# Regrouping small matmuls in a two-layer attention trunk on one core: compression in one group, compressed scores by pairs of heads, narrow value products, a split output projection

## The chip, the core and the metric

The kernel runs on one core of a Trainium2 chip. TensorE (PE) multiplies matrices; VectorE (DVE), ScalarE (ACT) and GpSimd (POOL) do the element-wise work; SyncE (SP) issues most of the DMA transfers from queues that keep their order. The metric is the device time of one execution in microseconds (us), as the median of several runs.

## What is computed

The reference is a two-layer decoder trunk in float32 for 512 tokens of width 1024. Each layer projects its normalised input once and runs two attention mixers side by side, forgetting attention (FoX, 8 heads) and native sparse attention (NSA, 8 query heads over 2 kv heads), mixes them with per-channel gates, and ends in a squared-ReLU MLP. Cut to what the change touches:

```python
def compress_blocks(t, pos_emb, w1, b1, w2, b2):        # NSA: one key (value) per block of 32 tokens, step 16
    blocks = t[:, :, idx, :] + pos_emb
    flat = blocks.reshape(B, G, nc, CMP_BLOCK * dh)      # 2048 long; w1 is 2048 x 256
    return jax.nn.gelu(flat @ w1 + b1) @ w2 + b2

def fox_attention(q, k, v, log_f):                       # per head: causal, with a forget bias
    s = einsum(q, k) * scale + ci[..., :, None] - c[..., None, :]
    s = jnp.where(kpos[None, :] <= qpos[:, None], s, -jnp.inf)
    return softmax(s) @ v

# NSA, per query head: probabilities over the compressed blocks, over selected blocks, over a window
p_c = softmax(where(cmp_end <= qpos, einsum(q, kc) * scale, NEG_BIG)) * valid_c
...
y_a = from_heads(o_a) @ w_o_fox
y_b = from_heads(g0 * o_c + g1 * o_s + g2 * o_w) @ w_o_nsa
x = x + (sigmoid(gate_a) * y_a + sigmoid(gate_b) * y_b) @ w_out
```

## The kernel before

All activations are kept transposed: features on the 128 partitions, the 512 tokens along the free axis. A float32 product is made of three TensorE products of a type called fp32r, in `gemm` (lines 243 to 245): both operands are split into a high part (rounded by ACT) and a low part (the rest, by DVE), and high x high, high x low and low x high are summed in one bank of PSUM. Weights come as 512 KB transfers (`fetch`, L201) and are split by `convert` (L217 on ACT, L218 on DVE). The inputs `uh`, `ul` come from `make_u` (L265 on ACT, L266 on DVE); the sums of squares for the norm are made by `sumsq` (squares on ACT at L274, sums on POOL at L284) and finished in `rstd` (L298, L315), with plain float32 products.

A layer has stages: token projections (values and gates, L357 to L359), FoX attention, NSA attention, output projection, mix, MLP. In an attention stage `attend` walks through units, one for each head (FoX) or for each head and branch (NSA). A unit has the steps scores, transposes and values, and between steps the next products of a filler generator are issued, so that TensorE has projections to do while ACT and DVE make the softmax. The filler of FoX (`fill1`) holds the FoX projections of later pairs of heads, the projections of `kc` and `vc`, then `compress` alternating step by step with the remaining projections. The filler of NSA (`fill2`) holds gated output projections, `cmp_gen` (the compressed scores and probabilities) and the last query projections. In which order the instructions of each engine then stand is decided by a scheduler from the recorded program; each engine and each queue works through its order strictly.

- `compress`: the windows of `kc` and `vc` are copied into tiles `ca`, 16 row groups each; w1 of each is loaded by 8 transfers of 256 KB (L651, on SP's queue) into tiles of the tags `oh` and `ol`. Key and value products run in the two column halves of the array, so the tile of a product is 128 x 64 with 256 columns (L665); they are plain float32 and take two instructions each. The 32 products of a layer are made in chunks of 4 steps `jj` (8 products), with other work of the filler between chunks. The result goes through gelu and w2, and ends in the key block `kcz` (L712, L713) and the value block `vz`.
- `q_pair` and `k_pair`: `hilo` splits the scaled queries or keys of two heads into `hla` (high and low); transfers on SP (L397, L401, L410, L419) put them into `kda`, `q2a` and `qx` so that one product of 128 rows holds the high part of a head against high and low. POOL clears parts of `qx` (L417, L418).
- `cmp_probs` (L732): the compressed scores of the four heads of a kv head go to four groups of 32 rows in one PSUM bank. `kcz` holds the 32 block keys with zeros around; a shifted view places them in the rows of head r. Each head takes two products of 512 columns: 8 for a kv head.
- `values` of FoX (L490): the probabilities, transposed into blocks of 128 x 128, high part (`pth`) and low part (`ptl`), times the values `vf`. Of the four key blocks b, block 0 meets 512 query columns, block 1 384, block 2 256, and block 3 only the last 128; the tile of the third group holds 128 zero columns in front of block 3 (cleared by DVE at L471, L472), so that its product has 256 columns:

```python
todo = [(0, 0, 0, 512), (1, 1, 0, 384), (2, 2, 256, 256), (3, 2, 0, 256)]
```

- `out_half` and `out_pair` (L508, L509) gather the outputs of a pair of heads and split them into `oh`, `ol`; for NSA these are the inputs `yb[p]` of the output projection, `half(1, m, w)` for m = 0 to 7, four pairs of heads p each.

Of the kernel before, what the change touches and what calls it, by code (L numbers as in the profile page):

```python
# [11 lines left out]
F32 = mybir.dt.float32  # L12
# [7 lines left out]
T = 512  # L20
# [123 lines left out]
class Body:  # L144
# [259 lines left out]
    def q_pair(self, x, fox=False):  # L404

        hl = self.hilo(x, 0.125)
        q2 = self.t("q2", [128, 2, T], F32R)
        for e in range(2):
            for f in range(2):
                self.nc.sync.dma_start(q2[f * 64:(f + 1) * 64, e].bitcast(F32),  # L410
                                         hl[e * 64:(e + 1) * 64, f].bitcast(F32))
        if not fox:
            return q2
        qx = []
        for e in range(2):
            t = self.t(("oh", "ol")[e], [128, T], F32R, name="qx")
            self.nc.gpsimd.memset(t[64:128].bitcast(F32), 0.0)  # L417
            self.nc.gpsimd.memset(t[64:66].bitcast(F32), 1.0)  # L418
            self.nc.sync.dma_start(t[:64].bitcast(F32), hl[e * 64:(e + 1) * 64, 0].bitcast(F32))  # L419
            qx.append(t)  # L420
        return q2, qx
# [32 lines left out]
    def transposes(self, u):  # L454
# [3 lines left out]
        for g in range(3):  # L458
            ps = self.p("PT")
            if g < 2:  # L460
                todo = [(i, g) for i in range(g, NB)]
            else:
                todo = [(3, 3), (2, 2), (3, 2)]
# [4 lines left out]
            o = 0  # L468
            if g == 2:
                o = 128  # L470
                nc.vector.memset(h[:, :128].bitcast(F32), 0.0)  # L471
                nc.vector.memset(lo[:, :128].bitcast(F32), 0.0)  # L472
            nc.scalar.copy(h[:, o:o + n], ps[:, :n])
            nc.vector.tensor_sub(lo[:, o:o + n], ps[:, :n], h[:, o:o + n].bitcast(F32))
# [3 lines left out]
    def values(self, u):  # L478
        nc = self.nc
        if u.get("first", True):  # L480
            u["O"][0] = self.p("O")
        O = u["O"][0]
        first = u.get("first", True)
        pt = u["pt"]
        last = u.get("last", True)
        todo = [(0, 0, 0, 512), (1, 1, 0, 384), (2, 2, 256, 256), (3, 2, 0, 256)]
        for b, g, o, n in todo:
            v = u["v"](b)
            for f in range(2):
                nc.tensor.matmul(O[:, T - n:], v, pt[g][f][:, o:o + n],  # L490
                                 start=first and b == 0 and f == 0, stop=last and b == 3 and f == 1)
            yield
        if "after" in u:
            u["after"]()
# [132 lines left out]
    def compress(self, kc, vc, small, l):  # L627
# [3 lines left out]
        for x, pos in ((kc, "pos_k"), (vc, "pos_v")):  # L631
# [11 lines left out]
            yield  # L643
        hp = self.p("O")
        self.held = self.bank_o
        loaded = deque()

        def load(c):
            for i in range(2 if c < 8 else 0):
                raw = self.t(("oh", "ol")[i], [128, T], name="w1")  # L650
                nc.sync.dma_start(raw, a["w1"][l, i, c].rearrange("p j m -> p (j m)"))  # L651
                loaded.append(raw)

        load(0)
        load(1)
        for c in range(0, 8, 2):
            load(c + 2)
            yield
            load(c + 3)
            yield  # L660
            w = [loaded.popleft() for _ in range(4)]
            for j in range(4):
                jj = 2 * c + j
                for i in range(2):
                    nc.tensor.matmul(hp[64 * i:64 * i + 64, :256], A[i][jj // 8][:, jj % 8],  # L665
                                     w[j // 2 * 2 + i][:, j % 2 * 256:(j % 2 + 1) * 256],
                                     start=jj == 0, stop=jj == 15)
            yield
            yield
# [42 lines left out]
        nc.scalar.copy(self.kcz[:, :, 0, 96:128], k2)  # L712
        nc.vector.tensor_sub(self.kcz[:, :, 1, 96:128], k2, self.kcz[:, :, 0, 96:128].bitcast(F32))  # L713
# [10 lines left out]
    def cmp_probs(self, hk, q2):  # L724
# [4 lines left out]
        for r in range(4):  # L729
            q = q2[2 * hk + r // 2][:, r % 2]  # L730
            for f in range(2):
                nc.tensor.matmul(sc, self.kcz[:, hk, f, 96 - 32 * r:224 - 32 * r], q,  # L732
                                 start=r == 0 and f == 0, stop=r == 3 and f == 1)
# [41 lines left out]
    def setup(self, first):  # L775
# [13 lines left out]
        self.kcz = t[:, 512:1408].rearrange("p (h f n) -> p h f n", h=2, f=2)  # L789
# [71 lines left out]
    def layer(self, l, u):  # L861
# [49 lines left out]
        st = {}  # L911
# [7 lines left out]
        def fox_unit(h):  # L919
            p, e = divmod(h, 2)  # L920
            un = dict(q=lambda: st["qa", p][0][:, e], qx=lambda: st["qa", p][1][e], k=lambda: st["ka", p][e], O=[None],
# [3 lines left out]
            def after():  # L925
                if e == 0:
                    st["oa", p] = self.t("zz", [128, T], name="o")
                self.out_half(un["O"][0], st["oa", p], e)
                if e == 1:
                    st["oa", p] = self.out_pair(st["oa", p])  # L930
# [8 lines left out]
        def qproj(p):  # L939
            return proj(12 + p, ("qb", p), lambda ps: self.q_pair(self.roped(ps)))  # L940

        def cmp_gen(hk):
            yield from self.cmp_probs(hk, [st.get(("qb", p)) for p in range(4)])
# [101 lines left out]
        for m in range(8):  # L1045
            if m % 2 == 0:
                w = self.weights(a["wo"][l, 1, m // 2].rearrange("p i c -> p (i c)"))
            run(half(1, m, w))
# [456 lines left out]
```

## Time and profile before

| | us |
|---|---|
| three runs | 1526.11, 1525.25, 1525.11 |
| median | 1525.25 |
| the profiled execution, whole | 1525.23 |
| its span in the trace | 1523.5 |
| busy TensorE, DVE, ACT, POOL | 1508.0, 1099.1, 809.8, 192.1 |
| granted TensorE clock, mean | 0.998 of full speed |

The span runs from the first to the last recorded instruction of the profiled execution; what lies around it is the rest of that execution's own time. TensorE instructions overlap in the trace: the recorded duration of one reaches into the next, so the time that a stream of them takes is read from the starts. A row such as "93.99 1.94 PE L665 ... x14" is a run of 14 instructions that starts at 93.99 us and is 1.94 us long. In brackets at the end of a row stand the idle time before it and what ended that.

### The profile page before, as it was taken

How to read it: one execution, taken by the hardware profiler on the slowest of the kernel's cores; microseconds unless marked ns; L12 is line 12 of the kernel's file. 1: busy time of each engine (PE TensorE's matmuls, PEld its weight loads, DVE VectorE, ACT ScalarE, POOL GpSimd, SP SyncE). 2: the span in 40 equal slices, each digit the busy share in tenths (PEclk: the TensorE clock that was granted, in tenths of full speed). 3: DMA queues.
4: the chain of work that ended last, by engine and by line, in shares of the span. 5: the costliest groups of instructions: out<-in, count | busy, mean ns of one | idle time of the engine just before them, and what ended most of it. 6: DMA issues, size and time to landing. Idle time of an engine off the chain costs nothing.

```text
span 1523.5 us, 21173 instructions
## 1 busy us (share of the span) xinstructions
PE 1508.0 (99%) x7696; PEld 1263.1 (83%) x7696; DVE 1099.1 (72%) x2124; ACT 809.8 (53%) x1530; POOL 192.1 (13%) x184
## 2 busy tenths in 40 slices
PE   9999999999999999999999999999999999999997
PEld 8878888887888888888888788888878888888897
DVE  4678988777478787775647799787674979766762
ACT  6365656554454655555435556555544636555553
POOL 4000000000300222112310000000012003122122
PEclk9999999999999999999999999999999999999999
DMA  7655522217324455421546552321462245545121
GB/s 260 166 146 142 146 73 84 70 66 224 120 97 137 140 146 142 140 77 63 173 152 167 160 131 85 96 69 60 135 187 97 98 152 146 146 126 150 50 83 56
DMA packets 67576, 188.82 MB, mean 124 GB/s; under 512 B 8560, under 2 KB 9968, under 8 KB 67472
## 3 DMA queue, kind: packets, MB, share of 16 engines
q1 hardware_dynamic: 56672, 168.31, 34.8%
q0 software_dynamic: 6912, 12.59, 5.0%
q10 hardware_dynamic: 3888, 6.58, 1.2%
q8 instruction: 60, 0.98, 0.3%
q14 instruction: 44, 0.36, 0.1%
HBM read 147.53 MB, written 4.19 MB: 100 GB/s over the span
## 4 chain that ended last, share of the span: by engine, by line
PE 87%; DVE 3%; ACT 2%; issue 1%; DMA 1%; POOL 0%; DVEq 0%; SPq 0%; POOLq 0%; ACTq 0%
PE ps_mm L243 12%; PE ps_mm L244 12%; PE ps_mm L245 12%; PE ps_O L1399 3%; PE ps_S L1399 3%; PE ps_PT L243 3%; PE ps_PT L244 3%; PE ps_PT L245 3%; PE ps_mm L1399 3%; PE ps_PT L1399 2%; PE ps_O L618 2%; PE ps_PT L592 2%; PE ps_S L243 2%; PE ps_S L244 2%; PE ps_S L245 2%; PE ps_O L244 2%
## 5 line engine op out<-in xcount | busy, mean ns | idle before, releaser
L217 ACT CAST wh<-raw 128x1024 fp32r<-128x1024 f32 (+2 forms) x187 | 192.3, 1029 | 279.7 <-issue 90.1
L218 DVE TENSOR_TENSOR wl<-raw,wh 128x1024 fp32r<-128x1024 f32 (+2 forms) x187 | 224.9, 1202 | 45.8 <-ACT wh L217 45.3
L243 PE MATMUL ps_mm<-uh,wh 128*128 128x512 f32 x512 | 204.4, 399 | 0.0
L245 PE MATMUL ps_mm<-uh,wl 128*128 128x512 f32 x512 | 202.3, 395 | 0.1
L244 PE MATMUL ps_mm<-ul,wh 128*128 128x512 f32 x512 | 202.1, 395 | 0.0
L243 PE MATMUL ps_mm<-oh,wh 128*128 128x512 f32 (+1 forms) x316 | 123.2, 391 | 2.0 <-ACT oh L508 1.7
L245 PE MATMUL ps_mm<-oh,wl 128*128 128x512 f32 (+1 forms) x316 | 122.4, 387 | 0.0
L244 PE MATMUL ps_mm<-ol,wh 128*128 128x512 f32 (+1 forms) x316 | 122.1, 386 | 0.0
L1389 DVE TENSOR_TENSOR sl<-raw,sh 128x512 fp32r<-128x512 f32 x120 | 97.1, 818 | 30.2 <-ACT sh L1388 30.1
L245 PEld LDWEIGHTS ps_mm<-uh,wl 128*128 128x128 f32 x512 | 96.3, 188 | 20.9 <-issue 0.8
L243 PEld LDWEIGHTS ps_mm<-uh,wh 128*128 128x128 f32 x512 | 96.7, 189 | 19.3 <-DVE wl L218 1.5
L244 PEld LDWEIGHTS ps_mm<-ul,wh 128*128 128x128 f32 x512 | 96.4, 188 | 16.6
L1362 POOL DMA_DIRECT2D raw<-raw x24 | 21.2, 885 | 696.4 <-DMA x<-xs 241.3
L596 ACT CAST pth<-ps_PT 128x384 fp32r<-128x384 f32 (+1 forms) x96 | 48.9, 512 | 64.4 <-PE ps_PT L592 64.2
L554 DVE CUSTOM_DVE_ANT_0 E<-ps_S,ct 128x384 f32<-128x384 f32 (+3 forms) x112 | 57.4, 515 | 31.7 <-PE ps_S L567 30.4
L555 ACT ACTIVATE E<-E,tiny 128x384 f32<-128x384 f32 (+3 forms) x112 | 65.6, 586 | 21.2 <-DVE tiny L554 20.7
L1388 ACT CAST sh<-raw 128x512 fp32r<-128x512 f32 x120 | 72.7, 618 | 2.0 <-PE ps_O L1399 0.7
L243 PEld LDWEIGHTS ps_mm<-oh,wh 128*128 128x128 f32 x316 | 59.3, 188 | 14.4 <-ACT oh L508 2.6
L245 PEld LDWEIGHTS ps_mm<-oh,wl 128*128 128x128 f32 x316 | 59.5, 188 | 12.2
L244 PEld LDWEIGHTS ps_mm<-ol,wh 128*128 128x128 f32 x316 | 59.5, 188 | 11.3 <-DVE ol L509 0.9
L243 PE MATMUL ps_PT<-oh,wh 128*128 128x512 f32 x172 | 67.7, 394 | 0.0
L245 PE MATMUL ps_PT<-oh,wl 128*128 128x512 f32 x172 | 67.3, 392 | 0.0
(443 smaller groups left out, 3938.3 us busy)
## 6 DMA issues: line engine op xcount, KB each, us to landing
raw<-wb SPq DMA_DIRECT2D x64, 512.0 KB
raw<-wup SPq DMA_DIRECT2D x64, 512.0 KB
raw<-wd SPq DMA_DIRECT2D x48, 512.0 KB
raw<-raw POOLq DMA_DIRECT2D x48, 256.0 KB, 3.7
w<-w SPq DMA_DIRECT2D x32, 256.0 KB
kda<-hla SPq DMA_DIRECT2D x32, 256.0 KB
q2a<-hla SPq DMA_DIRECT2D x64, 128.0 KB
raw<-wo SPq DMA_DIRECT2D x16, 512.0 KB
```

The lines of the kernel that those rows point to most:

```text
L217: nc.scalar.copy(h[:, :n], raw[:, :n])
L218: nc.vector.tensor_tensor(lo[:, :n], raw[:, :n], h[:, :n].bitcast(F32), op=OP.subtract)
L243: mm(ps, h[:, c], xh, start=start and i == 0, stop=False)
L244: mm(ps, h[:, c], xl, start=False, stop=False)
L245: mm(ps, lo[:, c], xh, start=False, stop=stop and i == ks - 1)
L554: nc.vector.tensor_tensor_reduce(e, ps, self.mask[:, T - n:], -1.0, BIG, OP.add, OP.min, mx)
L555: nc.scalar.activation(e, e, AF.Exp, bias=mx, scale=-1.0, accum_out=un["sm"][:, i:i + 1])
L592: nc.tensor.transpose(ps[:, j * 128:(j + 1) * 128], u["E"][i][:, b * 128:(b + 1) * 128], self.ident)
L596: nc.scalar.copy(h[:, e, :n], ps[:, :n])
L1388: nc.scalar.copy(h, src)
L1389: nc.vector.tensor_tensor(lo, src, h.bitcast(F32), op=OP.subtract)
L1399: mm = lambda o, w, x, **kw: self.nc.tensor.matmul(o, w, x, skip_group_check=True, **kw)
```

## The change

- `compress` loads the 8 steps of w1 into one tile of the tag `kk` (steps 0 to 3) and four of the tag `pt` (steps 4 to 7). Before the two loads of step c, POOL copies one column from the tile of step c - 2 (from `kc` for the first two) into the tile, so that the loads wait for those of step c - 2. All 32 products of a layer stand in one group, after the last load has been issued.
- `q_pair` keeps the split queries `hl` of NSA, and `cmp_probs` takes them: one product has the queries of two heads as its 128 rows, against a key block in which head 0's keys stand in rows 0 to 63 and head 1's in rows 64 to 127, at 32 columns of their own. Three products (high x high, high x low, low x high) for each of two pairs: 6 for a kv head. `kcz` is written by two ACT and two DVE instructions instead of one each, and has 192 columns for each of high and low, where it had 224.
- `values` of FoX: block 3 meets 128 columns, and there are no zero columns and no clearing. The order of the blocks in the third group is that of NSA.
- The output projection of NSA for m = 0 and m = 1: first the pairs of heads 0 to 2 of both, then pair 3 of both.

```diff
@@ -401,9 +401,11 @@
                 self.nc.sync.dma_start(kd[e][64:66, 1].bitcast(F32), self.CC[h:h + 33:32].bitcast(F32))
         return kd
 
-    def q_pair(self, x, fox=False):
+    def q_pair(self, x, fox=False, keep=None):
 
         hl = self.hilo(x, 0.125)
+        if keep is not None:
+            keep.append(hl)
         q2 = self.t("q2", [128, 2, T], F32R)
         for e in range(2):
             for f in range(2):
@@ -457,41 +459,26 @@
         u["pt"] = []
         for g in range(3):
             ps = self.p("PT")
-            if g < 2:
-                todo = [(i, g) for i in range(g, NB)]
-            else:
-                todo = [(3, 3), (2, 2), (3, 2)]
+            todo = self.PT_BLOCKS[g]
             for j, (i, b) in enumerate(todo):
                 nc.tensor.transpose(ps[:, j * 128:(j + 1) * 128], E[i][:, b * 128:(b + 1) * 128], self.ident)
             n = 128 * len(todo)
             h, lo = (self.t("t2", [128, T], F32R, name=k) for k in ("pth", "ptl"))
-            o = 0
-            if g == 2:
-                o = 128
-                nc.vector.memset(h[:, :128].bitcast(F32), 0.0)
-                nc.vector.memset(lo[:, :128].bitcast(F32), 0.0)
-            nc.scalar.copy(h[:, o:o + n], ps[:, :n])
-            nc.vector.tensor_sub(lo[:, o:o + n], ps[:, :n], h[:, o:o + n].bitcast(F32))
+            nc.scalar.copy(h[:, :n], ps[:, :n])
+            nc.vector.tensor_sub(lo[:, :n], ps[:, :n], h[:, :n].bitcast(F32))
             u["pt"].append((h, lo))
             yield
 
     def values(self, u):
         nc = self.nc
-        if u.get("first", True):
-            u["O"][0] = self.p("O")
-        O = u["O"][0]
-        first = u.get("first", True)
+        O = self.p("O")
         pt = u["pt"]
-        last = u.get("last", True)
-        todo = [(0, 0, 0, 512), (1, 1, 0, 384), (2, 2, 256, 256), (3, 2, 0, 256)]
-        for b, g, o, n in todo:
-            v = u["v"](b)
+        for b, g, o, n in ((0, 0, 0, 512), (1, 1, 0, 384), (2, 2, 0, 256), (3, 2, 256, 128)):
             for f in range(2):
-                nc.tensor.matmul(O[:, T - n:], v, pt[g][f][:, o:o + n],
-                                 start=first and b == 0 and f == 0, stop=last and b == 3 and f == 1)
+                nc.tensor.matmul(O[:, T - n:], u["v"](b), pt[g][f][:, o:o + n], start=b == 0 and f == 0,
+                                 stop=b == 3 and f == 1)
             yield
-        if "after" in u:
-            u["after"]()
+        u["after"](O)
 
     def out_half(self, O, o, e):
 
@@ -641,32 +628,22 @@
                         copy(t[half][r * 64:(r + 1) * 64, :, h, :31], v[h * 64:(h + 1) * 64, r, :, half:half + 31])
             A.append(t)
             yield
+        w = self.t("kk", [128, 4, 2, T], name="w1")
+        w = [w[:, c] for c in range(4)] + [self.t("pt", [128, 2, T], name="w1") for _ in range(4)]
+        for c in range(8):
+
+            nc.gpsimd.tensor_copy(w[c][:, :, :1], w[c - 2][:, :, :1] if c > 1 else kc[:, None, :1].to_broadcast([128, 2, 1]))
+            for i in range(2):
+                nc.sync.dma_start(w[c][:, i], a["w1"][l, i, c].rearrange("p j m -> p (j m)"))
+            yield
+            yield
         hp = self.p("O")
         self.held = self.bank_o
-        loaded = deque()
-
-        def load(c):
-            for i in range(2 if c < 8 else 0):
-                raw = self.t(("oh", "ol")[i], [128, T], name="w1")
-                nc.sync.dma_start(raw, a["w1"][l, i, c].rearrange("p j m -> p (j m)"))
-                loaded.append(raw)
-
-        load(0)
-        load(1)
-        for c in range(0, 8, 2):
-            load(c + 2)
-            yield
-            load(c + 3)
-            yield
-            w = [loaded.popleft() for _ in range(4)]
-            for j in range(4):
-                jj = 2 * c + j
-                for i in range(2):
-                    nc.tensor.matmul(hp[64 * i:64 * i + 64, :256], A[i][jj // 8][:, jj % 8],
-                                     w[j // 2 * 2 + i][:, j % 2 * 256:(j % 2 + 1) * 256],
-                                     start=jj == 0, stop=jj == 15)
-            yield
-            yield
+        for jj in range(16):
+            for i in range(2):
+                nc.tensor.matmul(hp[64 * i:64 * i + 64, :256], A[i][jj // 8][:, jj % 8],
+                                 w[jj // 2][:, i, jj % 2 * 256:(jj % 2 + 1) * 256], start=jj == 0, stop=jj == 15)
+        yield
         h = self.t("tmp", [128, 256])
         nc.scalar.copy(h, hp[:, :256])
         self.held = None
@@ -709,8 +686,11 @@
         nc.vector.tensor_mul(k, k, self.const("ccmp"))
         nc.vector.tensor_add(k, k, sh)
         k2 = k.rearrange("p (h n) -> p h n", h=2)
-        nc.scalar.copy(self.kcz[:, :, 0, 96:128], k2)
-        nc.vector.tensor_sub(self.kcz[:, :, 1, 96:128], k2, self.kcz[:, :, 0, 96:128].bitcast(F32))
+        for e in range(2):
+            s = slice(64 * e, 64 * e + 64)
+            z = self.kcz[s, :, :, 64 + 32 * e:96 + 32 * e]
+            nc.scalar.copy(z[:, :, 0], k2[s])
+            nc.vector.tensor_sub(z[:, :, 1], k2[s], z[:, :, 0].bitcast(F32))
         v = self.t("tmp", [128, 2, 64])
         b2v = small[:, OFF["b2v"]:OFF["b2v"] + 64]
         for hk in range(2):
@@ -721,16 +701,15 @@
             nc.scalar.copy(z[:, :, :64], v[s])
             nc.vector.tensor_sub(z[:, :, 64:], v[s], z[:, :, :64].bitcast(F32))
 
-    def cmp_probs(self, hk, q2):
+    def cmp_probs(self, hk, hl):
 
 
         nc = self.nc
         sc = self.p("S")
-        for r in range(4):
-            q = q2[2 * hk + r // 2][:, r % 2]
-            for f in range(2):
-                nc.tensor.matmul(sc, self.kcz[:, hk, f, 96 - 32 * r:224 - 32 * r], q,
-                                 start=r == 0 and f == 0, stop=r == 3 and f == 1)
+        for p in range(2):
+            k = self.kcz[:, hk, :, 64 - 64 * p:192 - 64 * p]
+            for i, (f, e) in enumerate(((0, 0), (0, 1), (1, 0))):
+                nc.tensor.matmul(sc, k[:, f], hl[2 * hk + p][:, e], start=p == 0 and i == 0, stop=p == 1 and i == 2)
         s = self.t("tmp", [128, T])
         nc.scalar.copy(s, sc)
         pt = self.p("PT")
@@ -786,7 +765,7 @@
         self.mask = self.const("mask")
         t = self.t("long", [128, 2048], F32R, name="kcz")
         self.CC = t[:40, :T]
-        self.kcz = t[:, 512:1408].rearrange("p (h f n) -> p h f n", h=2, f=2)
+        self.kcz = t[:, 512:1280].rearrange("p (h f n) -> p h f n", h=2, f=2)
         self.vz = t[:, 1408:1920].rearrange("p (h r d) -> p h r d", h=2, r=2)
         for t in (self.CC, self.kcz, self.vz):
             nc.gpsimd.memset(t.bitcast(F32), 0.0)
@@ -908,7 +887,7 @@
             nc.gpsimd.tensor_tensor(self.CRS[:, i], self.CRS[:, i], R, op=OP.mult)
         self.forget(z.rearrange("p b h -> p (b h)"))
 
-        st = {}
+        st, hl = {}, []
 
         def proj(i, key, fn, tag="mm"):
             def done(ps):
@@ -918,14 +897,14 @@
 
         def fox_unit(h):
             p, e = divmod(h, 2)
-            un = dict(q=lambda: st["qa", p][0][:, e], qx=lambda: st["qa", p][1][e], k=lambda: st["ka", p][e], O=[None],
+            un = dict(q=lambda: st["qa", p][0][:, e], qx=lambda: st["qa", p][1][e], k=lambda: st["ka", p][e],
                       ready=lambda: ("qa", p) in st and ("ka", p) in st,
                       v=lambda b: VF[b][:, h])
 
-            def after():
+            def after(O):
                 if e == 0:
                     st["oa", p] = self.t("zz", [128, T], name="o")
-                self.out_half(un["O"][0], st["oa", p], e)
+                self.out_half(O, st["oa", p], e)
                 if e == 1:
                     st["oa", p] = self.out_pair(st["oa", p])
             un["after"] = after
@@ -937,10 +916,10 @@
             yield from proj(2 * p + 1, ("qa", p), lambda ps: self.q_pair(self.scaled(ps), True), tags[1])
 
         def qproj(p):
-            return proj(12 + p, ("qb", p), lambda ps: self.q_pair(self.roped(ps)))
+            return proj(12 + p, ("qb", p), lambda ps: self.q_pair(self.roped(ps), keep=hl))
 
         def cmp_gen(hk):
-            yield from self.cmp_probs(hk, [st.get(("qb", p)) for p in range(4)])
+            yield from self.cmp_probs(hk, hl)
 
         def fill1():
             yield from fox_proj(1)
@@ -1045,7 +1024,15 @@
         for m in range(8):
             if m % 2 == 0:
                 w = self.weights(a["wo"][l, 1, m // 2].rearrange("p i c -> p (i c)"))
-            run(half(1, m, w))
+            if m == 0:
+                first = [self.p("mm") for _ in range(2)]
+                for part, kw in ((slice(0, 3), dict(stop=False)), (slice(3, 4), dict(start=False))):
+                    for i, ps in enumerate(first):
+                        run(self.gemm(ps, w, 4 * i + part.start, yb[part], ks=part.stop - part.start, **kw))
+            if m < 2:
+                st["y"] = first[m]
+            else:
+                run(half(1, m, w))
             t, y = st["gb", m], MA[m // 2][:, m % 2]
             nc.vector.scalar_tensor_tensor(t, t, 1.0, st["y"], op0=OP.add, op1=OP.mult)
             nc.vector.tensor_add(y, y, t)
```

## The prediction

> **What bounds the kernel now.** I read the page first, from the span down to the chain of work that ended last.
>
> ```profile
> span 1523.5 us, 21173 instructions
> ...
> PE 1508.0 (99%) x7696; PEld 1263.1 (83%) x7696; DVE 1099.1 (72%) x2124; ACT 809.8 (53%) x1530; POOL 192.1 (13%) x184
> ...
> PEclk9999999999999999999999999999999999999999
> ...
> PE 87%; DVE 3%; ACT 2%; issue 1%; DMA 1%; POOL 0%; DVEq 0%; SPq 0%; POOLq 0%; ACTq 0%
> ```
>
> TensorE (PE) is busy 99% of the span at full clock, and 87% of the chain is its own work; DVE has a quarter of the span free, ACT nearly half, POOL most of it. So an edit is worth what it takes from or adds to TensorE's stream of instructions, plus any gap that it opens or closes there. Work on DVE, ACT, POOL or the queues counts only if TensorE then waits.
>
> Next I read the groups of instructions, with different shapes kept apart, for the lines that the diff touches.
>
> ```profile
> L665 PE MATMUL ps_O<-w,ca 128*64 128x256 f32 x128 | 16.9, 386 | 0.0
> L490 PE MATMUL ps_O<-pth,vf 128*128 128x256 f32 x32 | 9.8, 307 | 0.0
> L490 PE MATMUL ps_O<-ptl,vf 128*128 128x256 f32 x32 | 9.2, 292 | 0.0
> L732 PE MATMUL ps_S<-q2a,kcz 128*128 128x512 f32 x32 | 8.3, 401 | 0.0
> L471 DVE MEMSET pth<- 128x128 f32 x16 | 2.6, 165 | 0.0
> ```
>
> The counts matter here: 128 compression instructions, 32 compressed-score products, 64 value products 256 columns wide (two of the four blocks of 16 heads, with two halves each). The mean durations do not: neighbours overlap, so a duration of 0.39 us is not a price. Prices I take from the TensorE timeline, as the distance from one start to the next.
>
> ```profile
> 87.05 0.65 PE L665 MATMUL ps_O<-w,ca 128*64 128x256 f32 x2
> 87.63 0.50 PE L245 MATMUL ps_mm<-uh,wl 128*128 128x512 f32 x1
> ...
> 93.99 1.94 PE L665 MATMUL ps_O<-w,ca 128*64 128x256 f32 x14
> 95.86 0.50 PE L243 MATMUL ps_mm<-uh,wh 128*128 128x512 f32 x1
> ...
> 104.46 0.39 PE L436 MATMUL ps_S<-kda,q2a 128*128 128x512 f32 x1
> 104.69 0.40 PE L439 MATMUL ps_S<-kda,qx 128*128 128x512 f32 x1
> 104.92 0.28 PE L490 MATMUL ps_O<-pth,vf 128*128 128x256 f32 x1
> 105.04 0.28 PE L490 MATMUL ps_O<-ptl,vf 128*128 128x256 f32 x1
> 105.25 1.95 PE L665 MATMUL ps_O<-w,ca 128*64 128x256 f32 x16
> 107.13 0.50 PE L243 MATMUL ps_mm<-uh,wh 128*128 128x512 f32 x1
> ...
> 127.09 1.95 PE L665 MATMUL ps_O<-w,ca 128*64 128x256 f32 x16
> ```
>
> A product of 512 columns takes 0.23 us (104.46 to 104.69), one of 256 columns 0.12 (104.92 to 105.04).
>
> **Compression in one group.** The product count stays; what goes is the cost of starting and ending pieces. A layer runs its 64 instructions in pieces of 2, 14, 16, 16 and 16: 0.58 us (87.05 to 87.63), 1.87 (93.99 to 95.86) and three times 1.88 (105.25 to 107.13), 8.09 in sum. Before a piece the preceding product keeps TensorE 0.21 (105.04 to 105.25) and not 0.12, so each entry costs 0.09 and five cost 0.45: 8.54 a layer. Inside a piece the last instruction alone takes 0.38 or so: the next 512-column product waits for two half-array products to drain. With 0.105 for each of the others (15 of them and 0.30 at the end make 1.88), a single group costs 64 x 0.105 + 0.20 + 0.09 = 7.01. That is 1.53 less a layer, 3.0 in both. Bounds: 1.0 a layer if the whole 1.88 scales with the count (64 x 0.1175 = 7.52), 1.8 if the group's own entry and exit hide as well (64 x 0.105 = 6.72).
>
> **Compressed scores.** Six products of 512 columns take the place of eight, for two kv heads in two layers: 8 fewer.
>
> ```profile
> 185.15 2.03 PE L732 MATMUL ps_S<-q2a,kcz 128*128 128x512 f32 x8
> 187.02 0.40 PE L567 MATMUL ps_S<-kka,q2a 128*128 128x256 f32 x2
> ```
>
> Eight take 1.87 us, 0.234 each, so 8 x 0.234 = 1.9 us go. The two extra ACT and two extra DVE writes of the key block come long before it, in the shadow of projections; ACT and DVE have room, so I cost them at nothing (some 0.25 us each if one were late).
>
> **No zero columns in FoX.** 32 products shrink from 256 to 128 columns, and 32 DVE memsets of 0.165 us go (row L471 and its twin, 5.3 us in all). DVE is not what TensorE waits for at these places, so the memsets are worth nothing. The products are the open question: no product of this operand type (fp32r) with 128 columns is in the trace. The narrow ones there are plain f32, in the rms code, where one product is two instructions:
>
> ```profile
> 28.76 0.95 PE L298 MATMUL ps_O<-tiny,acc 128*128 128x2 f32 x8
> 29.57 0.38 PE L357 MATMUL ps_mm<-wh,uh 128*128 128x288 f32 x1
> ...
> 31.77 1.05 PE L315 MATMUL ps_O<-tiny 128*128 128x128 f32 x8
> 32.58 0.38 PE L358 MATMUL ps_mm<-wl,uh 128*128 128x288 f32 x1
> ```
>
> Both take 0.101 us an instruction (0.81 / 8), at 2 columns as at 128, and so 0.20 a product. Three prices are possible. Lower end: the slope from 512 to 256 columns carried on, 0.12 - 0.055 = 0.064, saves 32 x 0.054 = 1.7 us. Middle: the 0.101 of a lone instruction as floor saves 32 x 0.017 = 0.5. Upper end: the narrow fp32r product loses its advantage over f32 and takes the 0.20 of the only 128-column product seen, which costs 32 x 0.082 = 2.6. I take the last: it is the row with the same width and the same four-byte operands, and that fp32r keeps its pace below 256 columns is shown nowhere. But it is a close choice.
> The Trainium skill ("TensorE: Matmul & The Clock Gate", section "Back-to-back issue gap") gives about 81 ns for a product of 128 columns in a stream of weight loads and products; by that the edit would save an estimated 32 x 0.037 = 1.2 us. The same sentence gives 131 ns for 512 columns, which the 0.23 us of row 104.46 contradicts, and it does not speak of this operand type, so it does not change my choice.
>
> **Last pair late.** The two programs issue the same TensorE order here: before too, the products of the first three pairs of heads for both m = 0 and m = 1 stand ahead of the first product of the fourth pair. The wait for the last pair therefore stays:
>
> ```profile
> 354.11 0.39 PE L245 MATMUL ps_mm<-oh,wl 128*128 128x512 f32 x1
> 354.70 0.62 ACT L508 CAST oh<-o 128x512 fp32r<-128x512 f32 x1 [0.76 <-DVE o L981]
> 355.37 0.73 PE L243 MATMUL ps_mm<-oh,wh 128*128 128x512 f32 x2 [0.87 <-ACT oh L508]
> ```
>
> It is 1.26 - 0.23 = 1.03 us a layer, and this part is worth 0.
>
> **Loads of the compression weights.** They go from the start of the layer into the FoX phase, each pair behind a POOL copy that waits for the load two steps earlier. At start-up this changes one gap:
>
> ```profile
> 15.61 1.29 POOL L284 TENSOR_TENSOR acc<-sq,acc 128x512 f32<-128x512 f32 x1 [0.28 <-ACT sq L274]
> 16.45 0.39 PE L359 MATMUL ps_PT<-wh,ul 128*128 128x512 f32 x1
> 16.93 0.72 ACT L265 ACTIVATE uh<-x,tiny 128x512 fp32r<-128x512 f32 x1 [1.40 <-POOL acc L284]
> 17.71 0.50 PE L357 MATMUL ps_S<-wh,uh 128*128 128x512 f32 x1 [0.87 <-ACT uh L265]
> ```
>
> TensorE loses 1.03 us (1.26 between starts, less 0.23) because the ACT scaling behind `uh` stands behind squares that wait for POOL. In the changed ACT order it stands ahead of them and needs only its x load, which in turn may come late behind a weight load on SP. I take half, 0.5 us, with bounds 0 and 1.1.
> In the FoX phase SP, POOL and DMA now hold these rows:
>
> ```profile
> raw<-raw POOLq DMA_DIRECT2D x48, 256.0 KB, 3.7
> ```
> ```profile
> 81.02 0.53 SPq L401 DMA_DIRECT2D kda<-kcz  x1
> ...
> 99.06 3.71 SPq L397 DMA_DIRECT2D kda<-hla  x4
> ...
> 107.73 0.47 SPq L410 DMA_DIRECT2D q2a<-hla  x1
> ...
> 118.99 1.89 SPq L397 DMA_DIRECT2D kda<-hla  x3
> ```
> ```profile
> 90.00:100.00 10.00, 10.00 (x56) 7.67 (x54) 7.88 (x22) 6.06 (x14) 0.00 (x0) 1.00 0.08 22
> ```
>
> By the changed SP order the chain begins behind the FoX loads of row 81.02, at about 82 us. A 256 KB transfer elsewhere lands 3.7 us after its issue; with two issues (0.53 each by row 81.02) and the copy a step is about 5 us, and the DMA engines are 8% busy there (22 GB/s, last figures of the window row), POOL is idle (its 0.00). Two chains run side by side (even and odd loads), so load 4 is issued at about 92, ahead of the keys of pair 2 (99.06, or 97 with 2.4 us of pieces gone before it). Loads 5 to 7 stand behind pair 2's loads, the last behind the first key load of pair 3: 118.99 less the 6.6 us of pieces gone is 112.4, so it lands at about 117. The group starts at 127.09 - 6.6 = 120.5 or later and needs load 7 six microseconds on. Hidden, with some 10 us to spare; cost 0.
>
> **The sum.** -3.0 - 1.9 + 2.6 + 0 - 0.5 + 0 = -2.8 us. The profiled execution took 1525.23 us (1.7 around its span), the median of the runs is 1525.25, so both give 1522.4.
>
> **The rivals.** *Narrow products at an instruction's floor.* The same sum with -0.5 for the values is -5.9: 1519.3. For it: fp32r is one instruction a product, and 2 columns cost what 128 do, so width does not set the 0.101. Against: the two f32 instructions could be so priced by something that an fp32r product also pays.
> *Everything at its best.* Values at 0.064 and the whole start-up gap: -3.0 - 1.9 - 1.7 - 1.1 = -7.7, 1517.5. Against: no instruction in the trace is spaced below 0.10 with a new 128-column weight.
> *SP blocked by the chain (slower).* SP issues in order. While load 4 waits for its POOL copy, the key, query and weight loads behind it wait too. Keys of pair 2 are due at 97 and SP is free from 102.8 to 107.7, which absorbs some 5 us. With a step of h, load 4 leaves at 82 + 2h: harmless up to h = 7.5, absorbed to 10, and beyond that TensorE waits 2(h - 10) a layer. To undo the gain and be slower by over 0.2% it takes 5.9 us, 2.95 a layer, h = 11.5; at h = 13 the loss is 12 us, 1534. For it: 16 transfers a layer with a dependence each, in a phase where TensorE needs those same queues. Against: 3.7 us landing and idle DMA engines; a step would have to be over twice my estimate.
> *The change does not do what it says.* So it is with the last pair; had it worked, both layers' 1.03 would go, 2.1 us more.
>
> **How the numbers follow.** About 0.2% (3.05 us) is what a measurement of this kernel can tell from no change, so faster means under 1522.2, slower over 1528.3. The forecast has 0.46, its own range 1520.5 to 1524.5 (compression 1.0 to 1.8 a layer, start-up 0 to 1.1, small waits at new places); it lies at the bound, so 0.19 of it is faster and 0.27 the same. The floor case has 0.30 (0.29 faster, 0.01 same), the best case 0.08 (faster), the blocked queue 0.16 (slower). That makes 0.56, 0.28 and 0.16. The range 1518.0 to 1525.5 takes in the first two cases, half of the third, and a chain that costs a little; it leaves out the blocked queue and the rest of the best case.
>
> **What would show it.** In the profile after: start-to-start distance of the 128-column value products, 0.20 or 0.10 (this alone decides between the two likeliest cases); one compression piece of 64 instructions a layer in about 6.9 us with no waits inside; 12 compressed-score products a layer where 16 stood; the gap at 16.45 short or gone; the gap before the fourth pair's products still 1.0; the key loads of pair 2 near 97. A TensorE gap released by SP or DMA between 95 and 130 us would make the forecast wrong.

## The result, and the profile after

| | before | changed |
|---|---|---|
| median (19 runs each), us | 1525.85 | 1529.11 |
| range, us | 1524.77 to 1526.60 | 1527.81 to 1531.42 |
| ratio of the runs, 95% interval | | 1.0023 (1.0016 to 1.0030) |
| profiled execution, us (span) | 1525.23 (1523.5) | 1530.61 (1528.8) |

The change costs 3.3 us where 2.8 us of gain were forecast: slower, by more than the interval, and outside the range. The profiled execution of the changed kernel lies 1.5 us above its median; places where executions of one kernel differ (start-up, one wait in the MLP) are not read as effects below.

The page of the changed kernel, first its parts 1 and 4:

```profile
PE 1505.8 (98%) x7688; PEld 1262.3 (83%) x7688; DVE 1095.6 (72%) x2094; ACT 811.6 (53%) x1532; POOL 194.6 (13%) x200
...
PE 83%; DVE 7%; ACT 4%; DMA 3%; issue 2%; SPq 0%; POOL 0%; DVEq 0%; ACTq 0%; POOLq 0%
```

TensorE has less to do (1505.8 us against 1508.0), and its share of the chain falls from 87% to 83%, while DVE's rises from 3% to 7%. The work did shrink, and waits more than took its place. TensorE's timeline shows the parts that went as summed, and those that did not:

```profile
125.95 0.39 PE L244 MATMUL ps_mm<-ul,wh 128*128 128x512 f32 x1
126.65 7.13 PE L644 MATMUL ps_O<-w,ca 128*64 128x256 f32 x64 [0.31 <-DVE o L489]
133.71 0.50 PE L245 MATMUL ps_mm<-uh,wl 128*128 128x512 f32 x1
...
147.07 0.28 PE L478 MATMUL ps_O<-ptl,vf 128*128 128x128 f32 x1
147.91 0.50 PE L243 MATMUL ps_mm<-uh,wh 128*128 128x512 f32 x1 [0.56 <-DVE tmp L371]
...
188.25 1.52 PE L712 MATMUL ps_S<-hla,kcz 128*128 128x512 f32 x6
189.61 0.40 PE L554 MATMUL ps_S<-kka,q2a 128*128 128x256 f32 x2
...
356.29 0.39 PE L245 MATMUL ps_mm<-oh,wl 128*128 128x512 f32 x1
357.55 0.73 PE L243 MATMUL ps_mm<-oh,wh 128*128 128x512 f32 x2 [0.87 <-ACT oh L495]
```

One group takes 7.06 us (6.92 and the entry were forecast), six score products 1.36 us (1.87 for eight before), and the wait for the last pair of heads is still there (1.26 between starts). But TensorE waits for DVE at the group's entry and again at 147, where it did not wait before. DVE's timeline around the group, first of the changed kernel, then the same place before:

```profile
128.06 0.69 DVE L496 TENSOR_TENSOR ol<-o,oh 128x512 fp32r<-128x512 f32 x1
135.17 0.29 DVE L444 CUSTOM_DVE_ANT_0 E<-ps_S,ct 128x128 f32<-128x128 f32 x1 [6.43 <-PE ps_S L441]
```
```profile
128.97 0.68 DVE L385 SCALAR_TENSOR_TENSOR hla<-tmp,hla 128x512 fp32r<-128x512 f32 x1
131.14 0.69 DVE L442 CUSTOM_DVE_ANT_0 E<-ps_S,ct 128x512 f32<-128x512 f32 x1 [1.49 <-PE ps_S L439]
```

During the group DVE has nothing to do for 6.43 us, because compression products give it no scores and no projections; beside the last piece of 16, in the kernel before, it was 1.49. The table by stretch says what that meets (columns: length; busy PE, PEld, DVE, ACT, POOL with counts; clock; DMA share; GB/s). Changed:

```profile
130.00:140.00 10.00, 10.00 (x69) 7.88 (x66) 3.55 (x9) 2.67 (x6) 0.00 (x0) 1.00 0.40 128
140.00:150.00 10.00, 9.35 (x52) 7.74 (x51) 8.46 (x29) 5.21 (x15) 0.00 (x0) 1.00 0.24 78
150.00:160.00 10.00, 10.00 (x52) 8.30 (x51) 9.89 (x24) 4.49 (x10) 0.00 (x0) 1.00 0.76 178
```

and before:

```profile
130.00:140.00 10.00, 10.00 (x55) 8.02 (x53) 8.01 (x22) 4.73 (x10) 0.00 (x0) 1.00 0.53 140
140.00:150.00 10.00, 10.00 (x53) 8.51 (x52) 9.68 (x31) 5.80 (x16) 0.00 (x0) 1.00 0.22 67
```

DVE does 3.55 us of work in ten instead of 8.01, and takes these arrears into a stretch in which it is soon nearly full (8.46, then 9.89 of 10). Whether this idle time is what costs TensorE time is the question of the experiments.

### The profile page after: what moved, and what is told of

Its sections match the earlier page's. It is cut to its first block, busy times and chain, and to the rows that moved or that the text cites. A ratio compares the mean times of both kernels' runs of the same rounds, so it can differ in the third digit from the quotient of the medians.

```text
span 1528.8 us, 21182 instructions
## 1 busy us (share of the span) xinstructions
PE 1505.8 (98%) x7688; PEld 1262.3 (83%) x7688; DVE 1095.6 (72%) x2094; ACT 811.6 (53%) x1532; POOL 194.6 (13%) x200
## 4 chain that ended last, share of the span: by engine, by line
PE 83%; DVE 7%; ACT 4%; DMA 3%; issue 2%; SPq 0%; POOL 0%; DVEq 0%; ACTq 0%; POOLq 0%
PE ps_mm L243 11%; PE ps_mm L244 11%; PE ps_mm L245 10%; PE ps_PT L244 3%; PE ps_PT L243 3%; PE ps_PT L245 3%; PE ps_O L1386 3%; PE ps_S L1386 3%; PE ps_mm L1386 3%; PE ps_O L605 2%; PE ps_PT L579 2%; PE ps_PT L1386 2%; PE ps_S L243 2%; PE ps_S L244 2%; PE ps_S L245 2%; PE ps_O L244 2%
```

## The experiments

Medians below stand beside 1525.8 to 1526.3 us for the kernel before on the same chips. Each trace is also cut at two products that all kernels share (at 62 and 220 us of the kernel before, 812 and 970 in layer 1), which takes in all of FoX and the start of NSA. For this stretch the table gives its length, TensorE's waits in it (the sum, over all distances between starts above 0.33 us, of what exceeds 0.23), and DVE's idle time, for layer 0 / layer 1.

| kernel | median, us | length, us | TensorE waits, us | DVE idle, us |
|---|---|---|---|---|
| before (pieces of 2, 14, 16, 16, 16) | 1525.85 | 157.97 / 158.04 | 1.8 / 1.0 | 24.5 / 24.8 |
| e1: changed, but pieces | 1522.67 | 156.73 / 157.12 | 1.6 / 1.2 | 24.6 / 25.0 |
| n4_early_2: changed, early group, early loads | 1526.20 | 158.73 / 158.41 | 4.0 / 3.1 | 26.0 / 26.3 |
| g1: changed, late group, early loads | 1525.69 | 159.00 / 159.32 | 4.1 / 3.7 | 27.9 / 26.8 |
| f1: late group, late loads, no chain | 1526.50 | 158.04 / 159.02 | 3.2 / 3.3 | 26.5 / 27.3 |
| changed (late group, chained loads) | 1529.11 | 159.91 / 160.10 | 4.8 / 4.1 | 28.2 / 28.4 |
| h3: pieces, at other places | 1533.62 | 162.31 / 162.43 | 5.4 / 4.6 | 30.5 / 31.5 |

**e1, the compression of before in the changed kernel** (`compress` from "loaded = deque()" to the last product taken back; everything else as changed).

> The changed kernel with the compression of before: w1 loaded by up to 16 unchained transfers in tiles oh and ol, products in pieces of 16 instructions between other work; the compressed scores by two heads, the narrow value products and the split output projection stay. Theory DVE: the single group of 64 instructions gives DVE nothing to do for some 6 us just ahead of the stretch where DVE is 95 to 99% busy, and this costs about 4.8 us a layer while the rest of the change works as summed. It expects 1525.85 - 1.9 (scores) - 1.7 (values at 0.06 us) = 1522.3 us, and no DVE idle time over 3 us between 125 and 140 us. Rival SP: the chained loads hold up SP's queue; it expects the same 1522.3. Rival cover: products taken away in FoX only uncover softmax waits; it expects 1525.5 or more.

1522.67 us, ratio 0.9980 (0.9971 to 0.9989): the new `compress` alone turns a gain of 3.2 us into a loss of 3.3. Beside its last piece DVE idles 1.46 us:

```profile
126.60 1.95 PE L652 MATMUL ps_O<-w,ca 128*64 128x256 f32 x16
128.48 0.50 PE L243 MATMUL ps_mm<-uh,wh 128*128 128x512 f32 x1
...
130.62 0.69 DVE L444 CUSTOM_DVE_ANT_0 E<-ps_S,ct 128x512 f32<-128x512 f32 x1 [1.46 <-PE ps_S L441]
```

**e2, the other way round** (the kernel before with the changed `compress` alone).

> The kernel before with the compression of the change alone (chained loads and one group of 64 instructions). Theories DVE and SP expect the whole loss here without the gains: 1529.1 + 1.9 + 1.7 = 1532.7 us, with DVE idle for 5 to 7 us beside the group. Rival cover expects about 1527, since part of the loss came from the other edits.

1533.20 us, ratio 1.0044 (1.0032 to 1.0057), close to the 1532.7 expected.

**e3 and e4, the narrow value products alone and the compressed scores alone.**

> The kernel before with the FoX value products of 128 columns alone (no zero columns, no memsets). Theories DVE and SP: 32 x (0.118 - 0.06) = 1.8 us less, 1524.0, and start-to-start 0.06 us for the first of each two. Rival cover: the time is not kept, 1525.5 to 1526.2.

> The kernel before with the compressed scores of two heads at a time alone (6 products for a kv head instead of 8). Theories DVE and SP: 8 x 0.234 = 1.9 us less, 1524.0, if DVE's bound at 140 to 200 us does not eat the first pair's share; with that 1524.9. Rival cover: 1525.4 or more.

1525.78 (0.9990 to 1.0008) and 1525.23 us (0.9987 to 1.0005): neither is told apart from no change. For e3 both the forecast's price and my expectation of 1524.0 were wrong; the time is the one that the rival (cover) expected. e4 lies between the two. Two narrow products start 0.06 and 0.11 us apart, but the product behind them pays; in the changed kernel, and before at a pair of 256 columns:

```profile
112.24 0.22 PE L478 MATMUL ps_O<-pth,vf 128*128 128x128 f32 x1
112.30 0.28 PE L478 MATMUL ps_O<-ptl,vf 128*128 128x128 f32 x1
112.41 0.45 PE L243 MATMUL ps_mm<-uh,wh 128*128 128x512 f32 x1
112.70 0.39 PE L244 MATMUL ps_mm<-ul,wh 128*128 128x512 f32 x1
```
```profile
118.29 0.28 PE L490 MATMUL ps_O<-pth,vf 128*128 128x256 f32 x1
118.40 0.29 PE L490 MATMUL ps_O<-ptl,vf 128*128 128x256 f32 x1
118.53 0.40 PE L243 MATMUL ps_mm<-uh,wh 128*128 128x512 f32 x1
118.76 0.40 PE L244 MATMUL ps_mm<-ul,wh 128*128 128x512 f32 x1
```

With the next product this is 0.46 us against 0.47: a pair of narrow products takes about 0.01 us less than a pair of wide ones, 0.2 us in all 16 pairs.

**e5 and e7, other cuts of the chained group** (e5: `piece(c - 3)` after the loads of c = 3, 5, 7, and `piece(6)` at the end; e7: three more `yield` after each four steps `jj`).

> The changed kernel with its chained loads, its tiles and its POOL copies, but the compression products in four pieces of 16 instructions, each as soon as its loads can be there (the third and fourth close together). Theory DVE: most of the loss goes, 1522.5 to 1524.5, since DVE gets work between the pieces. Rival SP (the chained loads hold up the queue): the loads are the same, so 1528 to 1530.

> The changed kernel with the group cut into four pieces of 16 instructions, the first where the group began and the others later, other work between; the loads are as in the change. Theory DVE: no idle DVE stretch of 6 us, so 1522.5 to 1525 (the compression's own DVE work comes some 10 us later, into the full stretch, but is not lengthened). Rival SP: 1528 to 1530.

1529.66 (1.0015 to 1.0034) and 1532.94 us (1.0032 to 1.0059). My theory (DVE) expected 1522.5 to 1525 and fell in the form it had: four pieces are not better than one group as such. The rival (SP) expected 1528 to 1530, which fits e5 but not e7. In e5 the queries of pair 2 also come late behind the chained loads on SP:

```profile
109.75 0.38 PE L464 MATMUL ps_PT<-tiny,E 128*128 128x128 f32 x2
110.91 0.47 PE L438 MATMUL ps_S<-kda,q2a 128*128 128x256 f32 x2 [0.77 <-DMA q2a<-hla]
```

**e6 and e8, DVE relieved** (`roped`: `nc.vector` becomes `nc.gpsimd` for the sine product; in the changed kernel and in e1).

> The changed kernel with one of the four DVE steps of the NSA rotation (the product of the shuffled copy with the sine table) on POOL: 0.69 us of DVE work less for each of six rotations a layer, four of them in the stretch where DVE is the bound, and the group kept whole. Theory DVE: up to 4 x 0.69 = 2.8 us a layer come back, so 1523.6 to 1527. If DVE is not the bound there: 1529 or, with POOL's longer product in the way, more.

> The changed kernel with the compression of before (pieces, unchained loads) and the sine product on POOL: the version that the theory points to. Theory DVE: below the 1522.7 us of the pieces alone, as the stretch from 140 to 185 us then no longer takes back what FoX saves (0.8 and 1.4 us a layer were taken back there): 1519.5 to 1521.5. Otherwise 1522.7 or more.

1531.59 (1.0027 to 1.0052) and 1527.01 us (0.9999 to 1.0017): both worse than without. POOL takes 1.29 us for what DVE did in 0.69. In e6 the sum on DVE waits for it in six of the twelve rotations, for 0.24 to 0.65 us. In e8 the sum does not wait. There TensorE waits 0.55 us for DVE's cosine product (L371), which frees its bank, and this product stands behind four writes of the key block (L712). The first of the four takes 1.39 us, while POOL's product runs; in e1 none takes over 0.29. First e8, then e1:

```profile
141.75 1.29 POOL L372 TENSOR_TENSOR tmp<-tmp,crs 128x512 f32<-128x512 f32 x1 [29.89 <-ACT kcz L711]
141.78 2.28 DVE L712 TENSOR_TENSOR kcz<-tmp,kcz 32x128 fp32r<-32x128 f32 x4
...
144.92 0.47 PE L243 MATMUL ps_mm<-uh,wh 128*128 128x512 f32 x1 [0.39 <-DVE tmp L371]
```
```profile
142.59 1.17 DVE L712 TENSOR_TENSOR kcz<-tmp,kcz 32x128 fp32r<-32x128 f32 x4
```

So these two do not settle whether DVE's amount of work is the limit: the step that went to POOL held up work that stayed on DVE.

**g1, f1 and f2, the group and its loads taken apart** (g1: all loads as before, then one group at the place of the change; f1: every copy reads `kc`, not the load two steps earlier; f2: it reads the load four steps earlier).

> The changed kernel with the loads of before (unchained, 16 tiles oh and ol, most of them issued at the start of the layer) but the products in one group of 64 at the place of the change. Separates the group from its loads. Theory group (products taken out from between the softmax steps and put together late leave DVE, then TensorE, idle): 1528 to 1530. Theory loads (SP's queue, POOL copies and the transfers in the FoX phase cost the time): 1522.5 to 1524.

> The changed kernel with all POOL copies reading kc, so that no load waits for another load, while loads, tiles and the group stay in the FoX phase. Theory group: 1528.5 to 1530, as with the chain. Theory loads, if it is the chain that holds SP: 1523 to 1526; if it is the mere place of the transfers: 1528.5 to 1530.

> The changed kernel with each POOL copy reading the load four steps earlier (kc for the first four), so that the loads go out in two waves and not in four; SP's order is nearly that of the version without the chain. If the waits of the chain cost the 2.6 us between 1526.50 (no chain) and 1529.11 (each load behind the one two steps earlier): between the two, 1526.5 to 1528.2. If it is the four-wave order that SP was given: 1526 to 1527. If neither, 1529.

1525.69, 1526.50 and 1527.49 us. For g1 and f1 neither theory's range was met; f2 lies where the theory of the chain's waits had it. From e1 on, the medians add up: late group +3.0 (with a later end of the compression, told under n4), loads moved into FoX +0.8, chain of two +2.6 (with f2 between, at +1.0). The 0.8 and the step to f2 cannot be told from nothing with these runs; the 2.6 just can (the intervals 0.9996 to 1.0014 and 1.0016 to 1.0030 do not meet). In g1 DVE idles 6.33 us beside the group. SP's queue, changed kernel and then f1:

```profile
86.29 0.99 SPq L637 DMA_DIRECT2D w<-w  x2
...
89.36 7.74 SPq L637 DMA_DIRECT2D w<-w  x8
97.30 0.33 SPq L201 DMA_DIRECT2D raw<-wb  x1
98.87 3.15 SPq L397 DMA_DIRECT2D kda<-hla  x4
```
```profile
86.46 4.41 SPq L637 DMA_DIRECT2D w<-w  x9
94.37 0.33 SPq L201 DMA_DIRECT2D raw<-wb  x1
95.95 3.80 SPq L397 DMA_DIRECT2D kda<-hla  x4
```

A step of the chain shows on POOL, at the first copy that waits for a load (issued at 86.29):

```profile
91.78 0.19 POOL L635 COPY w<-w 128x2 f32<-128x2 f32 x1 [12.21 <-DMA w<-w]
```

The chain keeps SP 7.74 us for eight loads, where nine took 4.41 without it. But the keys behind it are not later: from 78 to 165 us TensorE runs 2.9 to 3.0 us earlier in the f1 trace, and the keys 2.9. Of the 1.9 us by which f1's stretch is shorter in layer 0, 1.3 arise at 74.3, ahead of the first load of w1: there TensorE waits 1.19 us in the changed kernel, after ACT has waited 1.23 for a weight transfer. The same wait is not in layer 1, nor in f2. Since f1 and f2 were also given an order of the query loads of their own, how the 2.6 us arise stays open.

**h3, the pieces of e1 half a slot later** (two `yield` moved from behind a piece to ahead of it, and one more behind the last).

> The pieces of 16 with the loads of before as in the 1522.7 us version, but each piece about half a slot later, the last where the chained version with pieces had its last. Theory group: what matters is how the products lie between softmax steps and when the last is done; 1523 to 1526. Theory loads: the loads are unchained, so 1522.5 to 1523.5, and the 1529.7 us of pieces with chained loads came from the chain.

1533.62 us (1.0038 to 1.0064), the slowest of all and beyond either theory's range, with the loads of before and the same pieces. DVE's idle times over 2 us between 92 and 138 us, of which e1 has none:

```profile
102.06 0.56 DVE L444 CUSTOM_DVE_ANT_0 E<-ps_S,ct 128x384 f32<-128x384 f32 x1 [2.98 <-PE ps_S L441]
...
113.46 0.56 DVE L468 TENSOR_TENSOR ptl<-ps_PT,pth 128x384 fp32r<-128x384 f32 x1 [2.13 <-ACT pth L467]
...
124.10 0.69 DVE L468 TENSOR_TENSOR ptl<-ps_PT,pth 128x512 fp32r<-128x512 f32 x1 [2.28 <-ACT pth L467]
...
137.08 0.29 DVE L444 CUSTOM_DVE_ANT_0 E<-ps_S,ct 128x128 f32<-128x128 f32 x1 [2.57 <-PE ps_S L441]
```

The same four pieces (one of them with a few other products inside), put where DVE has just run out of input, cost 11 us more than in e1; part of it is that queries come late (TensorE waits 0.9 us for `q2a` at 136). So the place of such blocks can cost more than joining them; but h3 also has the later end of the compression, told next.

**n4, the group early** (loads of before; 2 or 6 steps of other work, then all 32 products, then the remaining steps).

> The changed kernel with the loads of before and all 32 compression products in one group, as early as the first piece of before (about 88 us in layer 0, not 127). Theory starve (a TensorE block that gives DVE no input leaves DVE idle, and this is lost where DVE is busy 95 to 99% soon after): the group's idle time lies ahead of 40 us in which DVE is busy 72 to 80% and can catch up, so less than the 3.0 us that the late group cost over pieces: 1521.5 to 1524.5. Theory late tail (a long group costs its own interruption wherever it stands): 1525 to 1527.

> The same with the group some 50 TensorE instructions later (about 96 us). Theory starve: little different from the early one, 1522 to 1525.5. Theory late tail: 1525 to 1527.

1526.20 and 1526.68 us (0.9989 to 1.0007, 0.9995 to 1.0013). The theory that DVE starves missed, with 1521.5 to 1524.5 and 1522 to 1525.5; the other, with 1525 to 1527, was met. The early group costs 3.5 and 4.0 us over e1, no less than the late one, and yet in n4_early_2 DVE never idles over 2.4 us beside it in layer 0 (2.9 in layer 1; 3.3 and 3.9 in n4_early_6). TensorE's waits (4.0 / 3.1 us) lie apart from the group:

```profile
92.61 7.13 PE L648 MATMUL ps_O<-w,ca 128*64 128x256 f32 x64
...
145.51 0.49 PE L243 MATMUL ps_mm<-uh,wh 128*128 128x512 f32 x1 [0.63 <-DVE tmp L371]
...
168.88 0.55 PE L464 MATMUL ps_PT<-tiny,E 128*128 128x128 f32 x3 [0.52 <-DVE ptl L468]
```

So "DVE idles ahead of its full stretch" is seen in the late group only. Something else is common to the group versions, and I had overlooked it: they also move the end of the compression (gelu and w2). From its copies to this end, `compress` has 16 steps (`yield`) in the kernel before and in e1, and 17 in every version with one group. The filler alternates its steps with those of the projections, so one step more lets six more projection products go ahead of the end. Counted from the cut at 62 us (layer 0):

| kernels | steps | projection products ahead of the end's product `ps_S<-G,small` | TensorE's wait at the 220th (layer 1: the 224th), us |
|---|---|---|---|
| before, e1, e3, e4, k1, n1, n2 | 16 | 201 | 0 |
| changed, g1, f1, f2, both n4, e6; and with pieces e5, h3 | 17 | 207 | 0.60 to 0.85 |
| e2 | 17 | 209 | 1.28 |

Row 145.51 is this wait. (e8, with 16 steps, waits 0.55 us there, for the reason told above; e7, with 26 steps, waits 2.4 us a layer further on.) So 1.2 to 1.6 us, over both layers, of the 3.0 to 4.0 that g1 and the n4 kernels lose against e1 stand at a wait that comes with the later end, with pieces too. No run has a group with 16 steps, or the pieces of e1 with 17, so how the loss divides between joining the pieces and the later end is open.

**n1 and n2, the split output projection** (n1: it alone on the kernel before; n2: e1 without it) **and k1** (e1 with the first three pairs of m = 0 to 3 ahead of the last, in the banks mm, mm, S, S).

> The kernel before with the split output projection of m = 0 and 1 alone. The order of the TensorE instructions there is that of before, so every theory expects no difference: 1525.5 to 1526.2, and the wait of 1.03 us a layer unchanged.

> The 1522.7 us version without the split output projection: narrow value products and scores by two heads, on the kernel before. The two alone brought 0.1 and 0.6 us; if the rest of the 3.2 us comes from the two together, 1522.7 again; if it comes from the split, 1525.2.

> The 1522.7 us version (pieces of before, the other edits of the change) with the first three pairs of heads of m = 0 to 3, not 0 and 1, ahead of the last pair, in two more PSUM banks: 18 products, 4.1 us, more in front of the wait of 1.03 us a layer. Every theory expects this wait to go: 1522.7 - 2.1 = 1520.6 us.

1525.92 us (0.9992 to 1.0010): the split is worth nothing, as forecast. 1523.13 (0.9974 to 0.9992): e1's gain does not come from it. k1 took the 1.03 us wait away and gained nothing, 1522.92 us where 1520.6 was expected: TensorE now waits for the split of the next weights, 0.4 us in each layer and 1.1 more in layer 1,

```profile
361.49 0.50 PE L245 MATMUL ps_mm<-oh,wl 128*128 128x512 f32 x1 [0.25 <-DVE wl L218]
...
1115.54 0.50 PE L243 MATMUL ps_PT<-oh,wh 128*128 128x512 f32 x1 [0.95 <-ACT wh L217]
```

e1 is the fastest of all, 3.2 us below the kernel before. A working that gives this sum is: 1.9 from the scores, 1.1 from pieces of 16, 16, 16, 16 (7.5 us a layer between starts, where 2, 14, 16, 16, 16 took 8.1), which its order of work happens to give, and 0.2 from the narrow products. The single edits do not bear it out: e3 has the same four pieces and gained 0.1 where this has 1.3, and e4 gained 0.6 of 1.9; together (n2) they gained 2.9. Both gaps are at the edge of the intervals, and why is open. (DVE is idle 0.9 and 1.3 us a layer longer in e3 than before, 25.4 and 26.1 us, but about as much of its work went with the memsets.)

## Why the prediction was wrong, point by point

- *Compression in one group, -3.0.* The failed step. The direct saving was there: 14.1 us for both groups and 16.2 for the pieces, 2.1 (the entries saved went on the group's own, which waits 0.47 and 0.61 us). What failed is the overlap: the forecast allowed for waits that the edit opens only as "small waits at new places" in its range, and had none in the sum. With the loads of before, one group costs 3.0 us (g1) to 4.0 us (n4_early_6) more than four pieces, at each of the three places tried, and TensorE's waits in the stretch rise from 1.6 / 1.2 (e1) to 4.1 / 3.7 us (g1). "An edit is worth what it takes from TensorE's stream" holds only while no wait opens. Part of these waits comes from the later end of the compression (1.2 us in g1), which the forecast did not look at either. That the pieces had covered softmax waits, TensorE working on them while DVE and ACT were busy, is my reading of the rest; it was not shown by itself. I listed DVE's and ACT's busy shares as room; the trace of before had the other view, DVE at 9.68 of 10 us soon behind the last piece.
- *Loads and chain, 0.* Wrong by 2.6, and perhaps by 0.8 more. The step of the chain was about as estimated (5.5 us from the load at 86.29 to the copy at 91.78), so the rival's threshold of 10 was never reached; the kernel with the chain is slower all the same. "About 10 us to spare" was right for the last load (issued at 117.65, needed at about 133). How the 2.6 us arise is not settled.
- *Narrow products, +2.6.* Mis-sized: -0.2, near the middle price (an instruction's 0.101 us as floor, -0.5). Width does not make fp32r slower here. The row taken has the right width, but it is plain f32 with two instructions a product; its price of one instruction was the nearer one.
- *Scores, -1.9.* The six products take 0.51 us less than eight each time (0.47 forecast); alone (e4) the edit gained 0.6 us, told apart neither from 0 nor from 1.9.
- *Last pair, 0.* Right; n1 and the row at 357.55.
- *Start-up, -0.5.* Not to be told: the gap moved from 16.45 to 19.69 us in the profiled execution, and start-up differs by over 1 us between executions.
- Had the narrow term been right, the forecast would have been 1519.6, farther off. The slower rival was on the list with 0.16, but with the wrong mechanism at its centre; no rival asked what the pieces had covered, or what stands behind the group.

## What to carry to other kernels

A block of filler can be worth two things: the time it takes, and the wait it hides. Before joining small blocks of the busiest engine's work into one, read at each of their places what the other engines do meanwhile, and who would wait if the block were gone; and see that what stands behind the blocks does not move with them, as the compression's end did here. Read a price over the neighbours too: two starts 0.06 us apart are no saving if the next start comes that much later. And a rise of TensorE's waits by a few us in a stretch of 160 decides over changes of this size, so compare waits in that stretch, not busy shares of the span.

## What the runs showed of the hardware

In e7 TensorE's products start 2.6 us apart at one place of each layer. Behind it, products of 512 columns start 0.43 us apart for some 3 us instead of 0.23, and the granted clock falls to 0.83 as a mean of ten microseconds, so these two waits cost more than themselves. The first rows are of layer 1, the ten microseconds of layer 0:

```profile
929.05 0.79 PE L245 MATMUL ps_mm<-uh,wl 128*128 128x512 f32 x1 [2.27 <-DVE wl L218]
929.64 0.63 PE L243 MATMUL ps_mm<-uh,wh 128*128 128x512 f32 x1
930.07 0.63 PE L244 MATMUL ps_mm<-ul,wh 128*128 128x512 f32 x1
```
```profile
170.00:180.00 10.00, 7.66 (x31) 6.12 (x30) 8.33 (x17) 5.28 (x12) 0.00 (x0) 0.83 0.73 194
```

In e8 a write of DVE that starts 0.03 us after a product of POOL ends 0.1 us after it: it takes 1.39 us instead of 0.28 (in layer 1, 1.29).
